# A decoder layer on one core: 192 gathered and 320 dense tokens instead of 128 and 384, with the key search cut into token halves

## The chip, the core and the metric

The kernel runs on one core of one Trainium2 chip. The metric is the device time of one execution in microseconds (us): the median of several runs, beside one execution that the hardware profiler recorded.

## What is computed

One decoder layer on 512 tokens of width 2048, in float32. Attention gives `h1`. The part that the change touches is the retrieval layer behind it: for each token and each of 8 heads two queries score 128 keys each, the best 16 of both are combined, and the best 16 sums name 16 of 16384 experts. A token so has 128 experts with gates.

```python
q = (xt @ wq).reshape(T, PEER_HEADS, 2, PEER_HALF)
s = jnp.einsum('thcd,hcnd->thcn', q, subkeys)
top_s, top_i = lax.top_k(s, PEER_TOPK)
...
u = u_tab[ec]
act = gelu(jnp.einsum('cd,chkd->chk', xc, u))
w = gc * act
return jnp.einsum('chk,chkd->cd', w, v_tab[ec])
```

Then `out = LayerNorm(alpha * h1 + peer + sigmoid(h1 @ ple_gate) * (p @ ple_proj))`.

## The kernel before

**Numbers.** Every product that has to be exact is done in three matmuls (`mm3`, lines 91 to 93): each operand is split into a rounded high part and the rest. `load_split` (81 to 88) does that for weights: SP loads a raw tile of 128x1024 (line 83), ScalarE writes the high part (86), VectorE or, where `eng` says so, GpSimd the low part (87). Raw, high and low tiles rotate over three buffers each. One such load feeds 24 matmuls of the dense stage.

**Tokens.** The 512 tokens stand in 4 blocks `tb` of 128. Block 0 is gathered: its experts' rows are fetched from the u and v tables by an indirect DMA, one expert of each of the 128 tokens at a time, so 128 gathers of u rows and 128 of v rows, each of 128 rows of 8 KB (`gather`, 700; `gather_step`, 708 to 722). VectorE consumes each of them in one instruction: the product with `h1` summed into a column of `act` (711), or the row times its weight added to an accumulator (721). The row tile has two buffers. Blocks 1 to 3 (384 tokens, `TD`) are dense: all 16384 experts are computed for them, with gates that are zero for the experts that were not chosen.

**Stages around the change.**
- `mix`, `norm1`, `spread` (445 to 497): the output matmuls with w_out in two token halves, the first norm, the transposes into the split operand `hs`, and on GpSimd the write of `h1` to DRAM.
- Projection (515 to 525): `p @ ple_proj` in 96 matmuls, written to DRAM as `projd`.
- Key search (586 to 594 and 543 to 584): for each of 16 key sets a query block of 48 matmuls over all 512 tokens, the scores (549), and on VectorE the two rounds of best eight (`top16`, 838 to 843), the sums of pairs and every fourth time the lookup of indices. `experts` (596) makes the softmax gates.
- Gate building (`dense_gates`, 610 to 644): for 24 groups of 16 tokens, one-hot tiles on VectorE, GpSimd and ScalarE, multiplied on TensorE, written to DRAM as `gd`.
- Gate projection (`ple_units`, 646 to 672): `h1 @ ple_gate` in 32 units of 24 matmuls each (512 columns). `fill(n)` (676) issues the next n units; such calls are spread over the end of the key search and the gate building, and `fill(32)` (691) issues what is left.
- Dense stage (763 to 821): 16 rounds g of 8 u blocks (`hp`, line 776, then gelu, gate and split at 779 to 785) and 8 c blocks (`vp`, 807, accumulated at 809 and 811). Every block takes 48 matmuls of 384 columns and ends with `gather_steps()` (727 to 732), which issues as many gather steps as keep them even over the first 240 of 256 blocks.
- The end (823 to 833): second norm, output.

Instructions are traced in the order of the program; the framework orders each engine's instructions by that order and by when its own timing says they are ready. Each engine then runs its queue in order. `issue_after` (730) places the gather's instruction behind the last low-half split on that split's engine.

## Time and profile before

| | us |
|---|---|
| median of 3 runs | 4052.41 |
| lowest and highest run | 4050.92, 4053.77 |
| span of the profiled execution | 4050.8 |
| TensorE busy in it | 3929.8 (97%) |
| VectorE busy | 2531.8 (63%) |
| ScalarE, GpSimd busy | 1318.5 (33%), 639.7 (16%) |

The profiled execution's own time is known by its span, from its first to its last instruction; it lies within 0.1% of the runs. PE is TensorE, PEld its weight loads, DVE VectorE, ACT ScalarE, POOL GpSimd, SP the engine that issues most loads. Busy shares are averages over stages with different limits, so a stage is read by its own window. Recorded matmuls overlap one another: their spacing is read from start to start. PEclk is the clock granted to TensorE as a share of 2.4 GHz.

### The profile page before, as it was taken

To read this page: it belongs to the slowest core of one execution; us is meant where nothing else is said; L and a number is where in the kernel's file an instruction comes from. 1 tells how busy PE (TensorE), PEld (TensorE's weight loads), DVE (VectorE), ACT (ScalarE), POOL (GpSimd) and SP (SyncE) were. 2 spreads that over 40 slices of the span, in tenths; PEclk is the share of its full clock that TensorE was granted. 3 is DMA by queue.
4 is the path that set the end of the run, shared out by engine and by line. 5 is a ranking of instruction groups with operands and counts; after the bars stand their busy time and mean duration, and the time that the engine had idled before them with its cause. 6 is when DMAs were issued, how large, how long until landed. Compare 5 with 4: busy or idle time off the path is not lost.

```text
span 4050.8 us, 52363 instructions
## 1 busy us (share of the span) xinstructions
PE 3929.8 (97%) x20841; PEld 3637.0 (90%) x20841; DVE 2531.8 (63%) x3817; ACT 1318.5 (33%) x1809; POOL 639.7 (16%) x563
## 2 busy tenths in 40 slices
PE   8999999999999897899999999999999999999996
PEld 7888887888887686789999999999999999999996
DVE  5444353322357699986767766666767667766756
ACT  3222233222234321575233223332333233322331
POOL 0000000000002442784111111111111111111101
PEclk9999999999999899899999999999999999999998
DMA  4222222222366422567877777777777777777744
GB/s 145 89 94 86 79 73 75 96 95 96 99 227 205 148 92 67 180 194 230 299 272 276 269 281 273 266 272 277 284 278 265 275 273 279 267 281 263 281 163 150
DMA packets 227588, 801.15 MB, mean 198 GB/s; under 512 B 20624, under 2 KB 71952, under 8 KB 191120
## 3 DMA queue, kind: packets, MB, share of 16 engines
q1 hardware_dynamic: 179856, 483.13, 35.1%
q0 software_dynamic: 40144, 282.09, 19.2%
q10 hardware_dynamic: 7344, 32.59, 2.1%
q8 instruction: 164, 2.69, 0.3%
q14 instruction: 80, 0.66, 0.0%
HBM read 755.78 MB, written 41.94 MB: 197 GB/s over the span
## 4 chain that ended last, share of the span: by engine, by line
PE 86%; DVE 8%; issue 2%; DMA 1%; ACT 1%; POOL 1%; POOLq 0%; DVEq 0%; ACTq 0%; SPq 0%
PE vp L92 9%; PE vp L91 9%; PE vp L93 9%; PE hp L93 9%; PE hp L92 9%; PE hp L91 9%; PE ps_g L92 3%; PE ps_g L91 3%; PE ps_g L93 3%; PE pg L641 2%; PE vps L91 1%; PE vps L92 1%; PE vps L93 1%; PE wo L92 1%; PE wo L93 1%
## 5 line engine op out<-in xcount | busy, mean ns | idle before, releaser
L93 PE MATMUL hp<-m_hi,wlo_u 128*128 128x384 f32 x2048 | 684.2, 334 | 2.5 <-DVE wlo_u L87 2.5
L93 PE MATMUL vp<-ah,wlo_vd 128*128 128x384 f32 x2048 | 685.9, 335 | 0.0
L91 PE MATMUL hp<-m_hi,whi_u 128*128 128x384 f32 x2048 | 684.2, 334 | 0.1
L92 PE MATMUL hp<-m_lo,whi_u 128*128 128x384 f32 x2048 | 684.2, 334 | 0.0
L92 PE MATMUL vp<-al,whi_vd 128*128 128x384 f32 x2048 | 672.4, 335 | 0.0
L91 PE MATMUL vp<-ah,whi_vd 128*128 128x384 f32 x2048 | 670.0, 335 | 0.0
L86 ACT ACTIVATE whi_vd<-raw_vd 128x1024 fp32r<-128x1024 f32 x256 | 271.7, 1061 | 744.5 <-PE vp L92 601.3
L87 DVE TENSOR_TENSOR wlo_u<-raw_u,whi_u 128x1024 fp32r<-128x1024 f32 x256 | 313.2, 1224 | 224.9 <-ACT whi_u L86 221.6
L86 ACT ACTIVATE whi_u<-raw_u 128x1024 fp32r<-128x1024 f32 x256 | 271.4, 1061 | 520.7 <-PE hp L92 401.0
L87 DVE TENSOR_TENSOR wlo_vd<-raw_vd,whi_vd 128x1024 fp32r<-128x1024 f32 x256 | 313.1, 1223 | 203.2 <-ACT whi_vd L86 203.0
L93 PEld LDWEIGHTS hp<-m_hi,wlo_u 128*128 128x128 f32 x2048 | 384.4, 188 | 3.4 <-DVE wlo_u L87 3.4
L91 PEld LDWEIGHTS hp<-m_hi,whi_u 128*128 128x128 f32 x2048 | 384.4, 188 | 0.4 <-ACT whi_u L86 0.4
L92 PEld LDWEIGHTS hp<-m_lo,whi_u 128*128 128x128 f32 x2048 | 384.4, 188 | 0.0
L93 PEld LDWEIGHTS vp<-ah,wlo_vd 128*128 128x128 f32 x2048 | 384.3, 188 | 0.0
L92 PEld LDWEIGHTS vp<-al,whi_vd 128*128 128x128 f32 x2048 | 383.1, 188 | 0.0
L91 PEld LDWEIGHTS vp<-ah,whi_vd 128*128 128x128 f32 x2048 | 382.9, 188 | 0.0
L721 DVE SCALAR_TENSOR_TENSOR accg<-vr,act,accg 128x2048 f32<-128x2048 f32 x128 | 300.3, 2346 | 14.4 <-DMA vr<-in_v_rows,eidx 9.7
L711 DVE SCALAR_TENSOR_TENSOR ur<-ur,h1g 128x2048 f32<-128x2048 f32 x128 | 291.9, 2285 | 15.1 <-DMA ur<-in_u_rows,eidx 15.1
L702 POOL DMA_INDIRECT vr<-in_v_rows,eidx x128 | 143.1, 1118 | 856.9 <-DVE accg L721 826.6
L702 POOL DMA_INDIRECT ur<-in_u_rows,eidx x128 | 140.7, 1100 | 837.6 <-DVE ur L711 821.1
L811 DVE TENSOR_TENSOR acc<-acc,vp 128x384 f32<-128x384 f32 x240 | 130.7, 550 | 131.1 <-PE vp L93 131.1
L91 PE MATMUL ps_g<-x_hi,whi_g 128*128 128x512 f32 x512 | 199.9, 391 | 0.0
(315 smaller groups left out, 6844.6 us busy)
## 6 DMA issues: line engine op xcount, KB each, us to landing
raw_u<-in_u_dense SPq DMA_DIRECT2D x256, 512.0 KB
raw_vd<-in_v_dense SPq DMA_DIRECT2D x256, 512.0 KB
raw_g<-in_w_z SPq DMA_DIRECT2D x64, 512.0 KB
raw_wo<-in_w_out SPq DMA_DIRECT2D x64, 512.0 KB
gd<-sg SPq DMA_DIRECT2D x24, 1024.0 KB
gl<-gd ACTq DMA_DIRECT2D x16, 1536.0 KB
raw_wq<-in_w_q SPq DMA_DIRECT2D x32, 512.0 KB
raw_pg<-in_w_gate SPq DMA_DIRECT2D x32, 512.0 KB
```

Source lines behind the costliest of these rows:

```text
L86: nc.scalar.activation(hi[:, :n], raw[:, :n], AF.Copy)
L87: last_lo[0] = (eng or nc.vector).tensor_sub(lo[:, :n], raw[:, :n], hi[:, :n])
L91: nc.tensor.matmul(ps, whi, mhi, start=start, stop=False, **kw)
L92: nc.tensor.matmul(ps, whi, mlo, start=False, stop=False, **kw)
L93: nc.tensor.matmul(ps, wlo, mhi, start=False, stop=stop, **kw)
L641: nc.tensor.matmul(ps[:, t1 * P:(t1 + 1) * P], o1[:, t1, :], o2, start=True, stop=True)
L702: nc.gpsimd.indirect_dma_start(out=row, out_offset=None, in_=table, in_offset=bass.IndirectOffsetOnAxis(ap=eidx[:, k:k + 1], axis=0))
L711: nc.vector.scalar_tensor_tensor(row, row, 1.0, h1g, op0=ALU.mult, op1=ALU.mult, accum_out=act[:, n:n + 1])
L721: nc.vector.scalar_tensor_tensor(state["acc"], row, act[:, k:k + 1], state["acc"], op0=ALU.mult, op1=ALU.add)
L811: nc.vector.tensor_add(acc[:, db, :], acc[:, db, :], ps[:, :TD])
```

## The change

64 tokens of block 1 (`GX`) leave the dense part and are gathered too. Each stands on two partitions: partition p holds the first half of its experts, partition 64 + p the second, so that 64 more gathers of u rows and 64 of v rows of the same size serve them (`HG` = 192 of each). The two partial sums are added at the end through a 64-row copy. The dense stage has 320 columns, the gate building 20 groups instead of 24.

The key search runs in two halves of 256 tokens, each with its own 16 query blocks of 48 matmuls, and so loads and splits the query weights twice. Gathers begin with half two: two steps behind each of its 16 query blocks, three with every second group of the gate building, the rest spread over the first 240 blocks of the dense stage. The projection moves from its own stage into the ends of the four ple columns, straight from the matmul's bank, and `projd` is gone. `fill` is called in half two, once, and in the gate building; what is left follows it.

```diff
-TD = T - P
+GX = 64
+T0 = P + GX
+TD = T - T0
 NB = TD // 16
+HG = P + P * GX // P
...
-    def column_block(src, act, name, nk=KB, eng=None, pre=()):
+    def column_block(src, act, name, nk=KB, eng=None, pre=(), ts=slice(0, T)):
         ps = bank(f"ps_{name}")
...
-                mm3(ps, hi[:, s], lo[:, s], act[0][:, kb, :], act[1][:, kb, :], kb == 0, kb == nk - 1)
+                mm3(ps[:, :cols], hi[:, s], lo[:, s], act[0][:, kb, ts], act[1][:, kb, ts],
+                    kb == 0, kb == nk - 1)
...
-    y = yp.tile([P, NT, D], F32, name="y")
+    h1g = hp.tile([P, D], F32, tag="h1g", name="h1g")
+    y = [h1g, hp.tile([P, D], F32, tag="h1x", name="y1"),
+         yp.tile([P, D], F32, name="y2"), yp.tile([P, D], F32, name="y3")]
...
+    pre_q = [load_split(w_q[0][:, u * 1024:(u + 1) * 1024], f"wq0_{u}") for u in range(2)]
+    norm1(1)
+    spread(1)
+    s3.close()
+    h1x = hp.tile([P, D], F32, tag="h1x", name="h1x")
+    for i in range(2):
+        nc.scalar.dma_start(h1x[i * GX:(i + 1) * GX, :], h1d[1][0:GX, :])
+
+    ep = s4.enter_context(tc.tile_pool(name="ep", bufs=2))
+    pj_hi = ep.tile([P, 2, T], F32R, name="pj_hi", bufs=1)
...
-    for c in range(4):
-        phi, plo = load_split(w_proj[c], f"pj{c}")
-        for tb in range(NT):
-            ts = slice(tb * P, (tb + 1) * P)
-            pj = bank(f"pj{c}_{tb}")
-            for k in range(2):
-                s = slice(k * 512, (k + 1) * 512)
-                mm3(pj, pj_hi[:, k, ts], pj_lo[:, k, ts], phi[:, s], plo[:, s], k == 0, k == 1)
-            o = xp.tile([P, 512], F32, tag="pj", name=f"pjs{c}_{tb}")
-            nc.scalar.activation(o, pj, AF.Copy)
-            nc.gpsimd.dma_start(projd[tb][:, c * 512:(c + 1) * 512], o)
-
-    pre_q = [load_split(w_q[0][:, u * 1024:(u + 1) * 1024], f"wq0_{u}") for u in range(2)]
-    norm1(1)
-    spread(1)
...
-    def key_scores(hc, q):
-        sk = qp.tile([P, P], F32, tag="sk", name=f"sk{hc}")
+    def key_scores(half, hc, q):
+        tbs = (2 * half, 2 * half + 1)
+        sk = qp.tile([P, P], F32, tag="sk", name=f"sk{half}_{hc}")
         nc.scalar.dma_start(sk, subk[hc])
-        pss = bank(f"pss{hc}")
-        for tb in range(NT):
-            c = slice(tb * P, (tb + 1) * P)
+        pss = bank(f"pss{half}_{hc}")
+        for i in range(2):
+            c = slice(i * P, (i + 1) * P)
             nc.tensor.matmul(pss[:, c], q[:, c], sk, start=True, stop=True)
-        s = qp.tile([P, T], F32, tag="s", name=f"s{hc}")
-        nc.scalar.activation(s, pss, AF.Copy)
-        for tb in range(NT):
-            top16(nc, s[:, tb * P:(tb + 1) * P], tv[:, tb, hc, :], ti[:, tb, hc, :])
+        s = qp.tile([P, 2 * P], F32, tag="s", name=f"s{half}_{hc}")
+        nc.scalar.activation(s, pss[:, :2 * P], AF.Copy)
+        for i, tb in enumerate(tbs):
+            top16(nc, s[:, i * P:(i + 1) * P], tv[:, tb, hc, :], ti[:, tb, hc, :])
         if hc % 2:
             h = hc // 2
-            for tb in range(NT):
+            for tb in tbs:
...
-    prev = None
-    for hc in range(16):
-        ps = column_block(w_q[hc], hs, f"wq{hc}", eng=nc.gpsimd if hc >= 3 else None,
-                          pre=pre_q if hc == 0 else ())
-        q = qp.tile([P, T], F32, tag="q", name=f"q{hc}")
-        nc.scalar.activation(q, ps, AF.Copy)
-        if prev is not None:
-            key_scores(*prev)
-        prev = (hc, q)
-
     def experts(tb):
-        fill(2)
-        gt = lg if tb == 0 else k2.tile([P, HK], F32, tag="gt", name=f"gt{tb}", bufs=3)
+        gt = kp.tile([P, HK], F32, name=f"gt{tb}") if tb else lg[:, 0:HK]
...
+    def gather_step(n):
+        if n < HG:
+            row = gather(n, u_rows, f"ur{n}")
+            nc.vector.scalar_tensor_tensor(row, row, 1.0, h1g if n < HK else h1x, op0=ALU.mult, op1=ALU.mult,
+                                           accum_out=act[:, n:n + 1])
+            return
+        if n == HG:
+            nc.scalar.activation(act, act, AF.Gelu)
+            nc.vector.tensor_mul(act, act, lg)
+            a0 = hp.tile([P, D], F32, tag="h1g", name="accg")
+            nc.gpsimd.dma_start(a0, base[0])
+            ax = hp.tile([P, D], F32, tag="h1x", name="accx")
+            nc.gpsimd.memset(ax[GX:P, :], 0.0)
+            nc.gpsimd.dma_start(ax[0:GX, :], base[1][0:GX, :])
+            state["acc"] = (a0, ax)
+        k = n - HG
+        row = gather(k, v_rows, f"vr{k}")
+        o = state["acc"][k >= HK]
+        nc.vector.scalar_tensor_tensor(o, row, act[:, k:k + 1], o, op0=ALU.mult, op1=ALU.add)
+
+    steps = [0, 0]
+
+    def gather_to(n):
+        while steps[1] < min(n, 2 * HG):
+            with tc.issue_after(last_lo[0].ins):
+                gather_step(steps[1])
+            steps[1] += 1
+
+    picks = {}
+
+    def half_keys(half, early):
+        prev = None
+        for hc in range(16):
+            ps = column_block(w_q[hc], hs, f"wq{half}_{hc}",
+                              eng=nc.gpsimd if hc >= 3 or half else None,
+                              pre=pre_q if not half and hc == 0 else (),
+                              ts=slice(half * 2 * P, (half + 1) * 2 * P))
+            q = qp.tile([P, 2 * P], F32, tag="q", name=f"q{half}_{hc}")
+            nc.scalar.activation(q, ps[:, :2 * P], AF.Copy)
+            if prev is not None:
+                key_scores(half, *prev)
+            prev = (hc, q)
+            if early:
+                gather_to(steps[1] + early)
+        if half:
+            fill(2)
+        key_scores(half, *prev)
+        for tb in (2 * half, 2 * half + 1):
+            picks[tb] = experts(tb)
...
-        tt = k2.tile([P, 3, P], F32, tag="tt", name=f"tt{tb}")
+        tt = k3.tile([P, 3, P], F32, tag="tt", name=f"tt{tb}", bufs=2)
         nc.vector.tensor_copy(tt, ps[:, 0:384].rearrange("p (a t) -> p a t", t=P))
-        for b in range(8):
+        for b in range(GX // 16 if tb == 1 else 0, 8):
             fill(1 if (tb * 8 + b) % 4 else 0)
-            sg = k2.tile([P, P, 16], F32, tag="sg", name=f"sg{tb}_{b}")
+            if (tb * 8 + b) % 2:
+                gather_to(steps[1] + 3)
+            sg = k3.tile([P, P, 16], F32, tag="sg", name=f"sg{tb}_{b}", bufs=2)
...
-            nc.sync.dma_start(gdw[:, :, (tb - 1) * 8 + b, :], sg.rearrange("p (g i) t -> p g (i t)", i=GE))
+            nc.sync.dma_start(gdw[:, :, tb * 8 + b - T0 // 16, :], sg.rearrange("p (g i) t -> p g (i t)", i=GE))
...
-                hi, lo = load_split(w_gate[c][:, u * 1024:(u + 1) * 1024], f"pg{c}_{u}",
-                                    eng=nc.gpsimd if c * 8 + u < 32 else None)
+                hi, lo = load_split(w_gate[c][:, u * 1024:(u + 1) * 1024], f"pg{c}_{u}", eng=nc.gpsimd)
...
+            phi, plo = load_split(w_proj[c], f"pj{c}")
             for tb in range(NT):
-                hr = k2.tile([P, 512], F32, tag="hr", name=f"hr{c}_{tb}")
+                ts = slice(tb * P, (tb + 1) * P)
+                pj = bank(f"pj{c}_{tb}")
+                for k in range(2):
+                    s = slice(k * 512, (k + 1) * 512)
+                    mm3(pj, pj_hi[:, k, ts], pj_lo[:, k, ts], phi[:, s], plo[:, s], k == 0, k == 1)
+                hr = ep.tile([P, 512], F32, tag="hr", name=f"hr{c}_{tb}")
                 nc.sync.dma_start(hr, h1d[tb][:, cs])
-                pj = k2.tile([P, 512], F32, tag="pj", name=f"pjr{c}_{tb}")
-                nc.sync.dma_start(pj, projd[tb][:, cs])
-                sg = k2.tile([P, 512], F32, tag="psg", name=f"psg{c}_{tb}", bufs=4)
+                sg = ep.tile([P, 512], F32, tag="psg", name=f"psg{c}_{tb}")
                 nc.scalar.activation(sg, ps[tb], AF.Sigmoid)
                 nc.vector.tensor_mul(sg, pj, sg)
                 nc.vector.scalar_tensor_tensor(sg, hr, ALPHA, sg, op0=ALU.mult, op1=ALU.add)
...
-    fill(2)
-    key_scores(*prev)
-    fill(1)
-    picks = [experts(0)]
-    ef = k2.tile([P, HK], F32, tag="ef", name="ef")
-    nc.vector.scalar_tensor_tensor(ef, picks[0][0], 128.0, picks[0][1], op0=ALU.mult, op1=ALU.add)
-    nc.vector.tensor_copy(eidx, ef)
-    for tb in range(1, NT):
-        picks.append(experts(tb))
+    half_keys(0, 0)
+    ef = k2.tile([P, 2, HK], F32, tag="ef", name="ef", bufs=1)
+    for tb in range(2):
+        nc.vector.scalar_tensor_tensor(ef[:, tb, :], picks[tb][0], 128.0, picks[tb][1], op0=ALU.mult, op1=ALU.add)
+    nc.vector.tensor_copy(eidx[:, 0:HK], ef[:, 0, :])
+    for i in range(P // GX):
+        ps_, ks = slice(i * GX, (i + 1) * GX), slice(i * GX, (i + 1) * GX)
+        nc.vector.tensor_copy(eidx[ps_, HK:HG], ef[0:GX, 1, ks])
+        nc.vector.tensor_copy(lg[ps_, HK:HG], picks[1][2][0:GX, ks])
+    half_keys(1, 2)
+    sq.close()
+    k3 = s4.enter_context(tc.tile_pool(name="k3", bufs=3))
     for tb in range(1, NT):
         dense_gates(tb)
     fill(32)
...
-    steps = [0, 0]
+    calls = [0, steps[1]]
 
     def gather_steps():
-        steps[0] += 1
-        while steps[1] < min(2 * HK, steps[0] * 2 * HK // (NG * 16 - 16)):
-            with tc.issue_after(last_lo[0].ins):
-                gather_step(steps[1])
-            steps[1] += 1
+        calls[0] += 1
+        gather_to(calls[1] + calls[0] * (2 * HG - calls[1]) // (NG * 16 - 16))
...
-                    mm3(ps[:, :TD], hi[:, s], lo[:, s], hs[0][:, kb, P:T], hs[1][:, kb, P:T],
+                    mm3(ps[:, :TD], hi[:, s], lo[:, s], hs[0][:, kb, T0:T], hs[1][:, kb, T0:T],
                         kb == 0, kb == KB - 1)
...
-                        nc.tensor.transpose(ps[:, i * P:(i + 1) * P],
-                                            acc[:, 2 * c - 2 + i, (tb - 1) * P:tb * P], ident)
+                        nc.tensor.transpose(ps[:k, i * P:(i + 1) * P],
+                                            acc[:, 2 * c - 2 + i, tb * P + lo_ - T0:tb * P + hi_ - T0], ident)
...
-            for c in range(4):
-                nc.vector.bn_stats(st2[:, 0, c, :], state["acc"][:, c * 512:(c + 1) * 512])
-            stats2(0, 1)
-            finish(state["acc"], 0, 0, D, False)
+            a0, ax = state["acc"]
+            up = rp.tile([P, D], F32, tag="row", name="up")
+            nc.sync.dma_start(up[0:GX, :], ax[GX:P, :])
+            nc.vector.tensor_add(ax[0:GX, :], ax[0:GX, :], up[0:GX, :])
+            for st, zt, dst in ((0, a0, out_rows[0]), (NT, ax[0:GX, :], out_rows[1][0:GX, :])):
+                for c in range(4):
+                    nc.vector.bn_stats(st2[:zt.shape[0], st, c, :], zt[:, c * 512:(c + 1) * 512])
+                stats2(st, st + 1)
+                finish(zt, st, dst, 0, D, False)
```

## Rows read from the trace of the kernel before

**Rows 1.** Windows by stage: us, busy us (instructions) per engine, PEclk, DMA share, GB/s
```profile
1313.70:1347.00 33.30, 29.20 (x131) 22.21 (x129) 18.10 (x34) 19.47 (x34) 8.91 (x17) 0.92 0.70 238
1347.00:1385.30 38.30, 30.44 (x110) 23.54 (x110) 25.72 (x20) 8.78 (x15) 20.93 (x7) 0.76 0.32 112
1385.30:1556.00 170.70, 165.20 (x771) 137.53 (x770) 158.19 (x648) 41.16 (x53) 68.13 (x28) 0.99 0.28 92
1556.00:1657.50 101.50, 75.82 (x315) 60.30 (x314) 100.66 (x340) 21.92 (x27) 30.62 (x15) 0.88 0.30 94
1657.50:1876.00 218.50, 204.99 (x1228) 181.70 (x1229) 178.81 (x453) 169.77 (x316) 189.76 (x219) 0.95 0.64 188
1900.00:1950.00 50.00, 47.43 (x269) 46.17 (x268) 38.55 (x42) 17.66 (x25) 11.44 (x8) 1.00 0.84 308
1950.00:3870.00 1920.00, 1920.00 (x11079) 1920.00 (x11078) 1339.19 (x1291) 590.54 (x688) 270.99 (x247) 1.00 0.76 274
```
**Rows 2.** Costliest groups of the page: busy us, mean ns, idle before and its releaser
```profile
L93 PE MATMUL hp<-m_hi,wlo_u 128*128 128x384 f32 x2048 | 684.2, 334 | 2.5 <-DVE wlo_u L87 2.5
```
**Rows 3.** Timeline of TensorE: start us, us (x8: all eight), line, operation, tile
```profile
900.03 0.39 PE L91 MATMUL ps_g<-x_hi,whi_g 128*128 128x512 f32 x1
902.75 0.39 PE L91 MATMUL ps_g<-x_hi,whi_g 128*128 128x512 f32 x1
...
2500.06 0.34 PE L91 MATMUL vp<-ah,whi_vd 128*128 128x384 f32 x1
2509.76 0.34 PE L91 MATMUL vp<-ah,whi_vd 128*128 128x384 f32 x1
...
1880.64 0.33 PE L91 MATMUL hp<-m_hi,whi_u 128*128 128x384 f32 x1
...
4018.64 1.47 PE L816 MATMUL zt<-ident,acc 128*128 128x128 f32 x12
...
1556.27 1.05 PE L549 MATMUL pss<-sk,q 128*128 128x128 f32 x8
```
**Rows 4.** Groups by line and form, VectorE, then one group of GpSimd
```profile
L87 DVE TENSOR_TENSOR wlo_u<-raw_u,whi_u 128x1024 fp32r<-128x1024 f32 x256 | 313.2, 1224 | 224.9 <-ACT whi_u L86 221.6 <-issue 2.9 <-PE hp L93 0.4
L721 DVE SCALAR_TENSOR_TENSOR accg<-vr,act,accg 128x2048 f32<-128x2048 f32 x128 | 300.3, 2346 | 14.4 <-DMA vr<-in_v_rows,eidx 9.7 <-DMA accg<-base 4.5
L711 DVE SCALAR_TENSOR_TENSOR ur<-ur,h1g 128x2048 f32<-128x2048 f32 x128 | 291.9, 2285 | 15.1 <-DMA ur<-in_u_rows,eidx 15.1
L811 DVE TENSOR_TENSOR acc<-acc,vp 128x384 f32<-128x384 f32 x240 | 130.7, 550 | 131.1 <-PE vp L93 131.1
L785 DVE TENSOR_TENSOR al<-a,ah 128x384 fp32r<-128x384 f32 x128 | 71.5, 559 | 70.5 <-ACT ah L784 70.5
...
L87 POOL TENSOR_TENSOR wlo_wq<-raw_wq,whi_wq 128x1024 fp32r<-128x1024 f32 x26 | 64.3, 2477 | 118.2 <-ACT whi_wq L86 97.7 <-PE pss L549 20.4
```
**Rows 5.** The gathered row tile ur
```profile
DMA to landing us min/median/max: 5.3/5.6/10.9
```
**Rows 6.** Timeline of GpSimd and of VectorE from 1918 us
```profile
1918.53 1.68 POOL L702 DMA_INDIRECT ur<-in_u_rows,eidx  x1 [6.29 <-DVE ur L711]
1929.40 1.68 POOL L702 DMA_INDIRECT ur<-in_u_rows,eidx  x1 [5.52 <-DVE ur L711]
...
1926.83 2.29 DVE L711 SCALAR_TENSOR_TENSOR ur<-ur,h1g 128x2048 f32<-128x2048 f32 x1 [2.14 <-DMA ur<-in_u_rows,eidx]
```
**Rows 7.** DMA queues from 2500 to 3500 us
```profile
q0 software_dynamic: 18582, 135.31, 37.6%
q1 hardware_dynamic: 34770, 126.59, 35.4%
```
**Rows 8.** Windows of ten microseconds, columns as in rows 1
```profile
1960.00:1970.00 10.00, 10.00 (x60) 10.00 (x59) 7.22 (x10) 2.44 (x3) 0.94 (x1) 1.00 0.93 360
```
**Rows 9.** Waits from 1380 to 1660 us: total us, times, longest
```profile
ACT h1g_gate L601 <- DVE h1g_gate L600: 26.7, 1, 26.7
```

103 lines of the change are left out of this document (47 added, 56 removed).

## The prediction

> **What bounds the kernel now.** I read the busy times of each engine by stage first [rows 1]. In the dense stage (first hp matmul at 1880.64, last transposes behind it at 4018.64 us [rows 3]) TensorE is busy in every microsecond at the full granted clock (1.00, the 2.4 GHz level), while VectorE is at 70% and the 16 DMA engines at 0.76. So TensorE alone sets the end there, and what an instruction of it takes is the price of the stage. The groups by line say the same from the other side: 2048 hp matmuls of one line waited 2.5 us in all [rows 2]. The stage ahead of it is another matter. From 1385 to 1657 us (key search) VectorE is busy 158.2 of 170.7 and 100.7 of 101.5 us, and TensorE is idle for 26 us of the second stretch at clock 0.88: VectorE bounds the search. In the gate building after it (1657.5 to 1876) TensorE (205 of 218.5 us), VectorE (179), ScalarE (170) and GpSimd (190) are all nearly full [rows 1]. So the change takes work from an engine that is the bound for 2138 us, and gives work to VectorE and the DMA queues, which bound elsewhere.
>
> **Part A, columns of the dense matmuls.** There are 12288 of them (6 groups of 2048, of which one stands in [rows 2]), 48 in each step of the stage (a u block or a c block, called a call below). Starts lie (902.75 - 900.03) / 12 = 226.7 ns apart at 512 columns and (2509.76 - 2500.06) / 56 = 173.2 ns at 384 [rows 3]. The slope is 53.5 / 128 = 0.418 ns a column, one column per 2.4 GHz cycle, over a fixed 13 ns. No 320-column matmul is in the trace. The line gives 146.5 ns; the bounds are 173.2 (no gain, if the weight load of each matmul were the floor) and 111 ns (8 matmuls of 128 columns, each with its own weights, start in (1.05 - 0.27) / 7 ns steps [rows 3], the 0.27 being one of them by itself). I take the line, since the two nearest rows lie on it. Saved: 26.7 x 12288 = 328 us; a call falls from 8.31 to 7.03 us.
>
> The Trainium skill (TensorE: Matmul & The Clock Gate, section Back-to-back issue gap) speaks against this: sustained spacing there is about 81 ns at 128 columns and 131 ns at 512, so by our estimate from that page 64 columns are worth 8.3 ns, part A 102 us, and the whole sum would end near 4080 us. The trace disagrees at 512 columns, with 226.7 ns, so the measurement is used.
>
> **Part B, more gathers in a shorter stage.** Steps go from 256 to 384 (192 for u, 192 for v). Two with each of 16 key blocks of half two and three with every second of the 20 gate groups make 32 + 30 = 62 before the dense stage; 322 are spread over 240 of its 256 calls. At 7.03 us a call these last 1687 us, so one gather is due every 5.24 us, where now it is 240 x 8.31 / 256 = 7.8 us.
> VectorE first. A call holds two splits (1.22 us), two 384-column operations (0.55; at 320 columns 0.48) and 1.34 gathers (2.29 and 2.35) [rows 4]: 2.45 + 0.96 + 3.1 = 6.5 of 7.03 us. It fits, with only half a microsecond left for waits.
> Then the gather's own chain. Two row buffers: gather n+2 is issued when VectorE has consumed n. At the quiet rate a gather lands 5.6 us after issue [rows 5], so two per 5.6 + 2.3 + 0.3 = 8.2 us, 4.1 each, and nothing is lost. But one stretch of this trace runs at nearly the new rate. From 1900 to 1950 us DMA is at 0.84 and 308 GB/s [rows 1], a gather issued at 1918.53 is consumed at 1926.83 after VectorE stood 2.14 us for it, and its buffer is issued again at 1929.40 [rows 6]: two gathers per 10.87 us, 5.44 each. TensorE lost 2.6 us in those 50 [rows 1]. That is the near row, and it says 322 x 5.44 = 1752 us, 65 more than 1687. The demand would be higher still: 322 gathers of 1 MiB and 240/256 of 268 MB of dense weights and 21 MB of gates are 609 MB in 1687 us, 361 GB/s, and the highest ten microseconds I found moved 360 at share 0.93 [rows 8]; queue by queue, 274 GB/s now cost 37.6 + 35.4% and a little [rows 7], which also scales to about 360 at full share. So I take 5.5 us: 1771, a loss of **84 us**. Ends: 0 (the quiet landing) and, with the longest landing of 10.9 us [rows 5], (10.9 + 2.6) / 2 = 6.75 us each, a loss of 487. Behind a late gather on VectorE's queue stand the next split's low half and the accumulation; TensorE, whose three weight buffers hold two blocks of 3.5 us, waits for the former.
>
> The Trainium skill (DMA: Bandwidth & Descriptors, section Specifications) gives about 358 GB/s as a core's HBM limit; by that alone part B would be 609 MB / 358 = 1701 us, a loss of 14, and the sum 3868 us. The ten-microsecond row at 360 agrees with it as a ceiling.
>
> **Part C, the stage ahead.** Steps, from 1313.7 us (end of the w_out matmuls) on:
> The projection (96 matmuls, 21.8 us by the 512-column pitch, with 16 evacuations and 16 GpSimd stores) leaves the front, where the second norm's transposes stood behind it on TensorE. Keys can start on VectorE at 1363 instead of 1385. The 16 reads of the projection on SP go too.
> Query matmuls: 1536 at 256 columns instead of 768 at 512. By the line 119.9 ns, 184 us instead of 174. VectorE's search covers the 10 us; without that cover they cost 10. 32 more weight splits on ScalarE and GpSimd (2.4 us each there [rows 4]) lie under the same cover.
> The search itself is the same work, 272 us [rows 1], now in two halves. Half two carries 32 gathers, 32 x 2.29 = 73 us more on VectorE. On GpSimd a gather waits for VectorE to free its row, with the low halves of later query weights behind it; they have a full key block of slack. Half one's end holds ScalarE for VectorE's softmax, as the 26.7 us wait does today [rows 9]: 0 to 27 us, taken as 8, since splits already done cover most.
> Gate building: 218.5 / 24 = 9.1 us a group now; VectorE's share is 7.45 and becomes 7.45 + 1.5 x 2.3 = 10.9, GpSimd's 7.9 becomes 9.5. I take 12 (that plus the present tenth of waits), 20 groups: 240 us; bounds 10.9 and 13.5.
> Gate projection (ple) units: 17 of 32 are issued by then, 15 remain, and two projection blocks: 17 x 24 x 226.7 ns = 92 us, with no gather beside them. Some will slip into TensorE's gaps between groups; I take 50, bounds 15 and 92.
> Sum: 1363 + 272 + 73 + 8 + 240 + 50 = 2006, against the dense stage's start at 1880.6: **+125 us**. Ends: 1941 (+60) and, without the earlier start, 1385 + 272 + 73 + 27 + 270 + 92 = 2119 (+238).
>
> **Part D, the end.** Finishing the 64 extra tokens adds a 64-row copy and some 10 us of VectorE, in the last 16 calls, which hold no gathers: taken as +5, between 0 and 15.
>
> **Sum.** Profiled span 4050.8 - 328 + 84 + 125 + 5 = 3937. The median of the runs is 1.6 above that span, so **3938 us**.
>
> **Rivals.**
> Forecast: faster, 3860 to 4020 us; 0.64.
> Gathers keep pace: B is 0 and C about +80 because ple units fill the gate building: 3808 us. For it: average DMA share 0.76 and 4.1 us quiet. Against: the 1900 to 1950 stretch. 0.18.
> Slower: the two-buffer gather chain becomes the bound. The point is 5.24 + (328 - 125 - 5) / 322 = 5.86 us a gather, a landing of 9.1 us. At 6.2 us B is 309 and the time 4163 us. For it: 8.3 us landings at only 308 GB/s; against: the peak of 360 was reached without TensorE standing. 0.12.
> The matmul's spacing does not follow its columns: A about 102 us, then 7.9 us calls, B 0, about 4080 us. Against: the 384- and 512-column rows. 0.03.
> Terms that cancel within 0.2% (8 us, what a measurement of this kernel can tell from no change): 0.03. That the early gathers do not come early is excluded by their place in VectorE's order; that they only stall it there is in C.
>
> So faster 0.64 + 0.18 = 0.82, same 0.03, slower 0.15. The range leaves out the lowest part of the second case and the slower cases but their edge: 3830 to 4055 us.
>
> **What the changed profile would show.** Right: dense matmuls 146 to 147 ns apart; the first hp matmul near 2006 us; waits of VectorE for gathers growing from 15.1 + 9.7 us [rows 4] to well over 100, TensorE idle between 50 and 120 us there, DMA share above 0.9. Wrong: spacing above 150 ns, a dense start beyond 2080 or before 1940, TensorE without idle time, or landings past 9 us.

## The result, and the profile after it

| | before | after |
|---|---|---|
| median of 4 runs, us | 4053.09 (4050.92 to 4054.92) | 4118.44 (4109.18 to 4138.49) |
| profiled span, us | 4050.8 | 4113.1 |
| first hp matmul | 1880.6 | 2107.9 |
| last transpose zt | 4019.8 | 4081.9 |

The ratio of the runs is 1.0167, 95% interval 1.0141 to 1.0193: slower by 1.7%, where 2.8% faster was forecast. The spans split the difference: the dense stage (first hp to last zt) fell from 2139.2 to 1974.0 us, 165 less; the stage ahead of it grew by 227 us; the end is the same within 1 us. The sum is 62 us.

TensorE in the dense stage of the changed kernel (timeline; to compare with [rows 3]):

```profile
2602.32 0.31 PE L96 MATMUL vp<-ah,wlo_vd 128*128 128x320 f32 x1
...
2604.96 0.31 PE L96 MATMUL vp<-ah,wlo_vd 128*128 128x320 f32 x1
```

Eighteen steps from start to start in 2.64 us are 146.7 ns each; the line through 512 and 384 columns had said 146.5. The matmuls gave what was hoped. What stands between them is in the costliest groups of the page (to compare with [rows 2]):

```profile
L96 PE MATMUL hp<-m_hi,wlo_u 128*128 128x320 f32 x2048 | 641.0, 314 | 43.5 <-DVE wlo_u L90 43.2
```

and in the waits of the dense stage from 2109 to 4022 us (total us, times, longest):

```profile
PE vp L96 <- DVE wlo_vd L90: 54.4, 31, 4.3
PE hp L96 <- DVE wlo_u L90: 43.2, 30, 4.2
...
DVE ur L607 <- DMA ur<-in_u_rows,eidx: 91.4, 59, 5.2
...
DVE accg L622 <- DMA vr<-in_v_rows,eidx: 64.9, 39, 4.7
DVE accx L622 <- DMA vr<-in_v_rows,eidx: 43.8, 31, 4.0
...
ACT whi_vd L89 <- DMA raw_vd<-in_v_dense: 382.3, 120, 8.6
...
ACT whi_u L89 <- DMA raw_u<-in_u_dense: 168.3, 94, 7.7
```

ScalarE's two waits for weights before, from 1881 to 4020 us:

```profile
ACT whi_vd L86 <- DMA raw_vd<-in_v_dense: 23.1, 6, 8.1
ACT whi_u L86 <- DMA raw_u<-in_u_dense: 11.9, 4, 6.0
```

TensorE waits about 110 us, nine tenths of it for low halves of weights from VectorE. VectorE waits 200 us for rows (25 before [rows 4]), and ScalarE 551 us for dense weights that have not landed (35 before). The stages, in windows (columns as in [rows 1]):

```profile
1347.00:1385.70 38.70, 7.11 (x39) 6.74 (x38) 18.77 (x16) 6.72 (x11) 14.43 (x6) 0.59 0.42 138
1385.70:1557.20 171.50, 143.49 (x1089) 140.76 (x1089) 162.56 (x566) 56.10 (x84) 102.37 (x42) 0.90 0.46 141
1557.20:1772.00 214.80, 111.89 (x670) 101.02 (x669) 212.32 (x486) 38.81 (x55) 100.85 (x59) 0.77 0.66 220
1772.00:2024.20 252.20, 182.94 (x950) 159.38 (x951) 211.85 (x440) 136.91 (x258) 221.62 (x210) 0.84 0.79 253
2024.20:2107.90 83.70, 83.70 (x372) 69.32 (x371) 14.56 (x16) 20.43 (x22) 28.90 (x16) 1.00 0.46 139
2107.90:4081.90 1974.00, 1860.08 (x12337) 1837.94 (x12335) 1572.00 (x1520) 646.24 (x777) 406.94 (x327) 0.98 0.87 321
```

In order: a stretch ahead of the keys in which TensorE does 7 us of work in 39; half one; half two with VectorE busy 212 of 215 us; the gates; a tail of 84 us in which TensorE is full and VectorE busy for 15; the dense stage. The border between the halves is drawn where half one's indices are done; by then VectorE has begun half two (40 of 64 MAX8 first selections lie ahead of it, and 32 are half one's), so the two are safest read as a sum, 386.3 us. In the search several of VectorE's operations are longer than before (groups from 1385 to 1775 us, mean ns after the busy us):

```profile
L581 DVE TENSOR_TENSOR oh<-oh,tf 128x512 f32<-128x512 f32 x32 | 45.4, 1442 | 0.0
...
L574 DVE CAST bcf<-bc 128x64 f32<-128x64 uint32 x16 | 18.3, 1149 | 0.0
L883 DVE FIND_INDEX8 ti<-tv,s 128x8 uint32<-128x128 f32 x64 | 17.5, 280 | 0.0
```

The same three before:

```profile
L582 DVE TENSOR_TENSOR oh<-oh,tf 128x512 f32<-128x512 f32 x32 | 32.5, 1033 | 0.0
...
L843 DVE FIND_INDEX8 ti<-tv,s 128x8 uint32<-128x128 f32 x64 | 17.4, 282 | 0.0
...
L575 DVE CAST bcf<-bc 128x64 f32<-128x64 uint32 x16 | 8.5, 532 | 0.0
```

The product oh went from 1033 to 1442 ns and the cast bcf from 532 to 1149, while FIND_INDEX8 stayed at 280. Not every product grew: oh from bcf and io went from 928 to 815. Beside them GpSimd ran 57 subtractions wlo_wq of 2539 ns (144 us) where it ran 26 (64 us).

### The profile page after: what moved, and what is told of

The parts are those of the page before. It is cut to its first block, busy times and chain, and to the rows that moved or that the text cites. A ratio compares the mean times of both kernels' runs of the same rounds, so it can differ in the third digit from the quotient of the medians.

```text
span 4113.1 us, 54046 instructions
## 1 busy us (share of the span) xinstructions
PE 3688.2 (90%) x21481; PEld 3403.4 (83%) x21481; DVE 2794.2 (68%) x3954; ACT 1308.4 (32%) x1812; POOL 914.5 (22%) x677
## 4 chain that ended last, share of the span: by engine, by line
issue 18%; PE 17%; DVE 14%; DMA 12%; POOL 5%; ACT 0%; POOLq 0%; DVEq 0%; ACTq 0%
DMA vr<-in_v_rows,eidx 6%; POOL ur L600 4%; PE hp L96 3%; PE hp L94 3%; PE hp L95 3%; PE vp L96 2%; PE vp L94 2%; DVE ur L607 2%; PE vp L95 2%; DMA ur<-in_u_rows,eidx 2%; DMA raw_vd<-in_v_dense 2%; DMA raw_u<-in_u_dense 1%; DVE oh L581 1%; DVE accx L622 1%; DVE wlo_u L90 1%
## 5 line engine op out<-in xcount | busy, mean ns | idle before, releaser
L96 PE MATMUL hp<-m_hi,wlo_u 128*128 128x320 f32 x2048 | 641.0, 314 | 43.5 <-DVE wlo_u L90 43.2
L96 PE MATMUL vp<-ah,wlo_vd 128*128 128x320 f32 x2048 | 612.4, 315 | 56.6 <-DVE wlo_vd L90 56.6
L94 PE MATMUL vp<-ah,whi_vd 128*128 128x320 f32 x2048 | 633.4, 314 | 13.5 <-ACT whi_vd L89 13.5
L94 PE MATMUL hp<-m_hi,whi_u 128*128 128x320 f32 x2048 | 638.1, 312 | 0.2 <-ACT whi_u L89 0.2
L95 PE MATMUL hp<-m_lo,whi_u 128*128 128x320 f32 x2048 | 637.7, 311 | 0.0
L95 PE MATMUL vp<-al,whi_vd 128*128 128x320 f32 x2048 | 632.4, 313 | 0.0
L600 POOL DMA_INDIRECT vr<-in_v_rows,eidx x192 | 244.2, 1272 | 851.6 <-DVE accg L622 533.2
L600 POOL DMA_INDIRECT ur<-in_u_rows,eidx x192 | 233.3, 1215 | 733.5 <-DVE ur L607 671.0
L607 DVE SCALAR_TENSOR_TENSOR ur<-ur,h1g 128x2048 f32<-128x2048 f32 x128 | 307.1, 2399 | 78.3 <-DMA ur<-in_u_rows,eidx 78.1
L689 PE MATMUL pg<-o,o 128*128 128x128 f32 x640 | 113.6, 336 | 150.5 <-ACT o L685 91.6
```

Source lines behind the costliest of these rows:

```text
L94: nc.tensor.matmul(ps, whi, mhi, start=start, stop=False, **kw)
L95: nc.tensor.matmul(ps, whi, mlo, start=False, stop=False, **kw)
L96: nc.tensor.matmul(ps, wlo, mhi, start=False, stop=stop, **kw)
L600: nc.gpsimd.indirect_dma_start(out=row, out_offset=None, in_=table, in_offset=bass.IndirectOffsetOnAxis(ap=eidx[:, k:k + 1], axis=0))
L607: nc.vector.scalar_tensor_tensor(row, row, 1.0, h1g if n < HK else h1x, op0=ALU.mult, op1=ALU.mult, accum_out=act[:, n:n + 1])
L689: nc.tensor.matmul(ps[:, t1 * P:(t1 + 1) * P], o1[:, t1, :], o2, start=True, stop=True)
```

## The experiments

The kernel before took 4050 to 4057 us beside each of them. The change, e6, e7 and g1 have four runs, the others one; the four of the change lie 29 us apart, so a smaller difference between single runs says little. The texts for d1, s1, e1 and e2 count 52 gathers ahead of the dense stage or 332 in it; the right numbers are 62 and 322. Their 542 us of waits for weights in the change are those of a shorter window than the 551 above. "Dense" is the first hp to the last zt.

| run | us | dense start | dense |
|---|---|---|---|
| the change | 4118.4 | 2107.9 | 1974.0 |
| d1 no row transfers in dense | 3954.7 | 2106.1 | 1815.5 |
| d2 no gather operation in dense | 3995.0 | 2100.1 | 1861.8 |
| d3 three row buffers | 4053.8 | 2102.3 | 1918.2 |
| d4 rows of half width | 3956.9 | 2107.0 | 1816.8 |
| d5 five weight buffers | 4151.6 | 2113.2 | 1898.6 |
| s1 no early gathers | 3929.1 | 1935.3 | 1965.0 |
| f1 gating early | 4069.0 | 2059.1 | 1976.6 |
| f2 no low query weights | 4027.0 | 2024.6 | 1968.7 |
| f3 early memory | 4114.7 | 2093.5 | 1988.1 |
| e1 all gathers in dense | 4144.7 | 1936.6 | 1994.3 |
| e2 the same, three rows | 3986.2 | 1938.7 | 2014.0 |
| e4 unsplit search, as e2 | 3936.8 | 1875.2 | 2028.6 |
| e5 as e4, gating early | 3933.4 | 1866.7 | 2033.6 |
| e6 as e5, four weight buffers | 3878.7 | 1867.7 | 1962.0 |
| e7 as e5, 32 added tokens | 3912.2 | 1897.8 | 1990.1 |
| g1 the change, 3 rows, 4 weights | 4019.1 | 2104.9 | 1881.2 |

### The dense stage: what holds TensorE

**d1.** In the dense stage the rows are two tiles of zeros:

```diff
     def gather(k, table, name):
+        if "still" in state:
+            return state["still"][k % 2]
```

> The changed kernel, with the row transfers of the dense stage left out: its 332 gather operations on VectorE run on two rows of zeros that stay in place, so the output lacks the gathered experts. Theory L (the dense stage waits because a gather has only two row buffers, and each row comes over 8 us after its issue): the wait is gone, the dense stage falls from 1973 us to 1810-1840 and the program to some 3960 us. Theory D (weights and rows together fill the DMA engines, and the weights come late): the same, and the waits of ScalarE for dense weights (542 us in the changed kernel) fall below 60 us. Theory V (VectorE, 80% busy, holds the weight halves back behind its 2.3 us gather operations): the dense stage stays above 1930 us and the program above 4070 us.

The window of the dense stage:

```profile
2106.10:3921.60 1815.50, 1809.02 (x12337) 1807.12 (x12335) 1555.74 (x1520) 642.73 (x777) 5.00 (x7) 1.00 0.53 165
```

1815.5 us, TensorE busy 1809: the floor of this stage. So the transfers cost 158.5 us, and VectorE at 1556 us of work does not bound it by itself: theory V in its plain form falls.

**d2.** The transfers stay, the operations on VectorE go (both `scalar_tensor_tensor` of `gather_step` are skipped in the dense stage).

> The changed kernel, with the gather operations on VectorE left out in the dense stage and the row transfers kept, so the output lacks the gathered experts. Theory L: a row buffer is free as soon as its row has landed, two gathers in 8 us or so, under the 5.2 us at which they are due, so the dense stage falls to 1810-1850 us and the program to some 3970 us. Theory D: the traffic is as before or comes faster, the dense stage stays above 1920 us, the waits of ScalarE for dense weights stay above 400 us. Theory V: VectorE falls to about half busy, the dense stage to 1810-1850 us, and TensorE's waits for VectorE there (98 us) go.

The windows of the dense stage and of 1000 us in it, then ScalarE's waits from 2101 to 3902 us:

```profile
2100.10:3961.90 1861.80, 1832.54 (x12336) 1810.32 (x12335) 879.92 (x1067) 645.42 (x776) 328.30 (x305) 1.00 0.87 330
2500.00:3500.00 1000.00, 984.00 (x6616) 970.34 (x6615) 461.04 (x554) 342.84 (x409) 232.95 (x215) 1.00 0.99 384
...
ACT whi_vd L89 <- DMA raw_vd<-in_v_dense: 429.3, 170, 8.0
...
ACT whi_u L89 <- DMA raw_u<-in_u_dense: 214.2, 107, 5.4
```

1861.8 us, between all the forecasts. ScalarE still waits 643 us for weights, yet TensorE waits only 27 us for low halves and high halves together, so late weights alone do little. The operations, and the waits for rows that stand before them on VectorE, cost the other 112 us; d2 takes away both and doesn't part them. That a late weight has no slack left to stand behind a gather operation is a reading that fits, not shown by itself. Rows and weights also ran at 384 GB/s for a whole millisecond, on the same two row and three weight buffers: the 321 GB/s of the change were not the most that the DMA engines can bring.

**d3.** A third row buffer in the dense stage:

```diff
-        row = rp.tile([P, D], F32, tag="row", name=name)
+        if "row" in state and k % 3 == 2:
+            row = state["row"].tile([P, D], F32, tag="row3", name=name)
+        else:
+            row = rp.tile([P, D], F32, tag="row", name=name)
```

> The changed kernel with a third row buffer for the gathers of the dense stage, everything else as it is. Theory L: a gather has half as much time again, VectorE's waits for rows (197 us) fall below 60 us and the dense stage falls by 80 us or more, to 1890 us or less; the program to some 4030 us. Theory D: the dense stage stays within 30 us of 1973 us, and the rows land later than before (10 us or more from issue) as three are under way. Theory V: the dense stage stays within 30 us of 1973 us too, with VectorE's waits for rows gone and TensorE's waits for VectorE still there.

56 us back, short of the 80 that theory L named. The waits of the dense stage in d3 (all of those for rows that are listed, then those for weights):

```profile
DVE ur L610 <- DMA ur<-in_u_rows,eidx: 5.5, 1, 5.5
...
ACT whi_vd L89 <- DMA raw_vd<-in_v_dense: 438.4, 165, 9.5
ACT whi_u L89 <- DMA raw_u<-in_u_dense: 281.8, 125, 7.3
```

The waits for rows are gone and those for weights grew from 551 to 720 us. So the third row gives back a third of the loss, and what is left (103 us) is a loss with late weights and without waits for rows.

**d4.** Each transfer brings 1024 columns; VectorE reads them twice, so its operation keeps its length (`table.rearrange("n (a w) -> (n a) w", w=1024)`, the row broadcast over two halves).

> The changed kernel with rows of half the width in the dense stage: each transfer brings 1024 columns of 128 rows, 0.5 MB and not 1 MB, and VectorE's operation reads them twice, so that it takes its 2.3 us; the output's gathered experts are wrong data. Without the transfers the dense stage took 1815 us, with them 1974. Theory D (bytes: weights and rows together need the DMA engines 0.87 of the time): 322 half rows take 170 MB off 602 MB, the dense stage falls to 1815-1850 us. Theory L (latency of two buffers): a landing of half the bytes comes in some 5 us and not 8, the stage falls as far. Theory Q (each gather costs by its 128 descriptors and its issue on GpSimd, and not by bytes): the stage stays above 1930 us. The waits of ScalarE for weights tell D from L: under D below 150 us, under L they stay near 540 us.

The window of d4's dense stage:

```profile
2107.00:3923.80 1816.80, 1809.66 (x12336) 1807.16 (x12335) 1558.31 (x1519) 643.44 (x777) 369.77 (x326) 1.00 0.77 257
```

and its waits there:

```profile
ACT whi_u L89 <- DMA raw_u<-in_u_dense: 18.0, 8, 3.2
ACT whi_vd L89 <- DMA raw_vd<-in_v_dense: 16.7, 7, 4.5
```

The floor again, with every gather issued and every operation of VectorE in place, and ScalarE's waits for weights down to 35 us, which theory D asked and theory L did not. So it is the size of the rows; their number, issue and descriptors on GpSimd (theory Q) cost nothing here. VectorE's waits for rows fell too, from 200 to 37 us; d4 doesn't tell whether the rows help as fewer bytes beside the weights or by landing sooner in their own chain.

**d5.** Two more buffers for raw weights, rows on two as before:

```diff
+        loads[0] += 1
+        if more[0] and loads[0] % 5 > 2:
+            raw = more[0].tile([P, 1024], F32, tag="raw2", name=f"raw_{name}")
+        else:
+            raw = wp.tile([P, 1024], F32, tag="raw", name=f"raw_{name}")
-        raw = wp.tile([P, 1024], F32, tag="raw", name=f"raw_{name}")
```

> The changed kernel with five buffers for the raw weights of the dense stage and not three, the rows on two as before. Theory P (the weights come late because a buffer of theirs is freed only by VectorE's low half, which stands behind gather operations that wait for rows, so that too few loads are under way): with two more loads ahead, ScalarE's waits for weights (542 us) halve and the dense stage falls by 40 us or more, to 1930 us or less. Theory D (the DMA engines are full and share themselves out between weights and rows): the rows land later in return, and the dense stage stays within 25 us of 1974 us.

The dense matmuls took 75 us less, and the program 33 us more. ScalarE's waits for weights fell from 551 to 26 us. Rows (q0) and weights (q1) that d5 moved from 2500 to 3500 us (packets, MB, share):

```profile
q0 software_dynamic: 23259, 169.31, 44.8%
q1 hardware_dynamic: 39879, 145.22, 41.1%
```

the tile accx of d5, whose row ends with the first and last start of its gather operations:

```profile
L628 DVE SCALAR_TENSOR_TENSOR accx<-vr,act,accx x64: 2275/2352/2355, 3747.2 to 4127.5; 128x2048 f32<-128x2048 f32 x64
```

and the queues in the changed kernel (to compare with [rows 7], where they were 135 and 127 MB):

```profile
q0 software_dynamic: 25019, 182.11, 48.8%
q1 hardware_dynamic: 37156, 135.30, 36.3%
```

In the same 1000 us the weights gained 10 MB and the rows lost 13: a row of 1 MiB every 5.76 us became one every 6.19, and the last gather operation started 116 us after the last transpose. Both theories are half right: more loads under way free TensorE (P), and the rows pay for it (D). The total was 328.8 MB in the change and 327.4 here. This is the rival's mechanism, the two-buffer chain as the end of the program, in the open.

### The stage ahead: where 227 us come from

**s1.** The early gathers are left out (`gather_to` counts them without issuing before the dense stage).

> The changed kernel with the 52 gathers ahead of the dense stage left out (transfers and VectorE operations; the output lacks these experts), the dense stage as it is. By the prediction's prices for them (73 us in the second half of the key search, and some 55 us of operations and waits in the gate building, where VectorE is 84% busy) the dense stage starts 90-130 us earlier than 2108, at 1980-2020 us. If they lie beside other work, it starts less than 30 us earlier. The tail of the token gating after the gates (84 us) stays in either case, and the dense stage takes 1973 us within 20.

Half one, half two, the gates and the tail of s1:

```profile
1385.90:1554.50 168.60, 144.83 (x1094) 142.10 (x1094) 158.91 (x567) 56.23 (x84) 102.92 (x42) 0.90 0.47 144
1554.50:1680.50 126.00, 108.02 (x660) 97.35 (x658) 125.93 (x419) 32.39 (x48) 60.96 (x25) 0.93 0.38 113
1680.50:1850.00 169.50, 154.50 (x948) 136.90 (x949) 140.88 (x379) 138.04 (x263) 148.06 (x181) 0.96 0.64 187
1850.00:1935.30 85.30, 85.30 (x378) 70.59 (x378) 14.54 (x16) 20.46 (x23) 29.39 (x17) 1.00 0.45 136
```

173 us earlier, more than expected. Half two is 126 us and not 215 (32 gathers, 89 us: 2.8 each), the gates 170 and not 252 (30 gathers, 83 us: 2.8 each). VectorE is full in half two (212 of 215 us), where an early gather so costs its whole operation and some waiting. In the gates VectorE is busy 212 and GpSimd, which issues the gathers, 222 of 252 us (141 and 148 of 170 in s1); which of them sets the price there was not separated. In the dense stage of the changed kernel it costs 158.5 / 322 = 0.5 us.

**e1, e2.** What the 62 cost when they are moved into the dense stage, on two and on three row buffers:

```diff
-    half_keys(1, 2)
+    half_keys(1, 0)
...
-            if (tb * 8 + b) % 2:
-                gather_to(steps[1] + 3)
```

> The changed kernel with no gather ahead of the dense stage: all 384 are spread over its 240 calls, on two row buffers. The run without early gathers started the dense stage at 1935 us, so this one does too, within 15. Theory L (each gather takes a place in the two-buffer chain, 5.76 us apart in the changed kernel): 384 of them need 2210 us, and the program takes some 4180 us. Theory S (a gather in the dense stage costs what it shares with the other work, (1974 - 1815) / 332 = 0.48 us, against 173 / 52 = 3.3 us ahead of it): the dense stage takes 1815 + 184 = 2000 us, the program some 3965 us.

> The same with a third row buffer in the dense stage. Theory S with the price of the run with three rows, (1918 - 1815) / 332 = 0.31 us a gather: dense stage 1935 us, program 3900 us. Theory D (weights and rows fill the DMA engines; 384 rows of 1 MB and the weights of 256 MB at the 331 GB/s that the run with three rows reached): 403 MB + 268 MB at 331 GB/s is 2030 us, program some 3990 us. Theory V (VectorE: 808 us of other work and 384 x 2.3 us are 1691 us, with waits for the weights between them): above 2030 us.

The last window of e1, from the last transpose to the end:

```profile
3930.90:4142.60 211.70, 0.45 (x3) 0.05 (x1) 124.28 (x83) 4.75 (x8) 58.30 (x47) 0.50 0.64 221
```

and its tile accx:

```profile
L622 DVE SCALAR_TENSOR_TENSOR accx<-vr,act,accx x64: 2276/2352/2402, 3791.8 to 4120.2; 128x2048 f32<-128x2048 f32 x64
```

TensorE's part of the stage took 1994 us, as theory S said to 6 us; the program took 4145, near theory L's 4180: TensorE is not held by a chain that is late, it ends and waits 212 us for it. With a third row the gathers keep up, the end is 31 us as ever, and the program is at 3986, 68 us below the kernel before. The dense stage is then 2014 us, near theory D's 2030 and far over theory S's 1935: its price of 0.31 us a gather did not carry from 322 gathers to 384.

**f2.** The low half of the query weights is left out (no `wlo_wq`, no third matmul for it).

> The changed kernel with the low half of the query weights left out (GpSimd's 57 subtractions of 2.5 us and the third matmul of each product; the queries lose low bits). Theory G (GpSimd's subtractions hold up VectorE's operations in the key search): the means of VectorE's operations in the halves fall to those of before (cand 612 ns from 797, oh 1033 from 1442, tf 599 from 1095), the first half takes 130-140 us and not 170, the dense stage starts 35-60 us earlier. If VectorE's operations are longer for another reason: the halves stay as they are, within 10 us.

Windows of f2, to the start of the keys and of its two halves:

```profile
1347.00:1367.10 20.10, 5.42 (x24) 5.16 (x25) 10.93 (x11) 7.43 (x12) 7.70 (x4) 0.62 0.64 213
1367.10:1505.00 137.90, 134.02 (x1092) 131.63 (x1092) 132.90 (x629) 80.84 (x116) 9.33 (x5) 0.99 0.79 258
1505.00:1676.40 171.40, 48.19 (x186) 37.78 (x186) 169.38 (x423) 15.49 (x22) 49.41 (x40) 0.65 0.67 227
```

and its groups from 1385 to 1775 us:

```profile
L585 DVE TENSOR_TENSOR oh<-oh,tf 128x512 f32<-128x512 f32 x32 | 20.4, 679 | 0.0
...
L887 DVE FIND_INDEX8 ti<-tv,s 128x8 uint32<-128x128 f32 x57 | 15.6, 284 | 0.0
...
L578 DVE CAST bcf<-bc 128x64 f32<-128x64 uint32 x16 | 5.0, 314 | 0.0
```

Half one is 137.9 us (171.5 in the change), the product oh 679 ns (1442), the cast 314 (1149), FIND_INDEX8 284: the operations lengthen when GpSimd works beside them, and only some kinds do. Of the 83 us by which the dense stage comes earlier, 77 lie in the two halves (309.3 us for 386.3), 19 in the start of the keys, and the gates and the tail take 12 back. This is the price of all 57 subtractions; the price of the 31 that the change added was not measured. The third matmul went too, but TensorE was not what half two waited for: it was busy 112 of 215 us in the change. The Trainium skill (SBUF — State Buffer, section Who interferes with whom) says that VectorE and GpSimd share one pair of ports under an exclusive lock, and that VectorE operations with two SBUF inputs, or in a two-port mode, contend for it. The rows agree: from f2 to the change the products of two tiles and the casts grow, and FIND_INDEX8 doesn't.

**f3.** The query tiles in memory that nothing earlier holds, the projection's input split later.

```diff
+    qp = s4.enter_context(tc.tile_pool(name="qp", bufs=2))
     s3 = ExitStack()
...
+            if not half and hc == 2:
+                ...
+                nc.scalar.activation(pj_hi, rv, AF.Copy)
```

> The changed kernel with the query tiles in memory that no earlier tile holds, and the split of the projection's input moved behind the third query block (and six and not eight buffers for the gates' second factor, to make room). Between the end of the mix and the first key operation on VectorE (1347 to 1386 us) TensorE is busy 7 us of 39 in the changed kernel. If ScalarE's wait for the memory of the freed rows makes that hole: keys on VectorE start at 1360-1368 us as the prediction had it, and the dense stage starts 15-25 us earlier than 2108. If the hole is the load and low half of the query weights behind the row spreading on GpSimd: it stays, within 5 us.

In the change ScalarE stood for memory that the store of the rows still held, in the waits from 1347 to 1386 us:

```profile
ACT pj_hi L530 <- DMA h1d<-y: 12.2, 1, 12.2
```

With f3 the keys start on VectorE at 1364.3 (1385.7 in the change; 1363 was predicted) and the dense stage at 2093.5, 14 us earlier. Memory is one part of the cause. The store was late because it stood on GpSimd behind a subtraction of query weights, in the change:

```profile
1367.90 2.34 POOL L90 TENSOR_TENSOR wlo_wq<-raw_wq,whi_wq 128x1024 fp32r<-128x1024 f32 x1 [9.88 <-ACT whi_wq L89]
1370.18 1.12 POOL L501 DMA_DIRECT2D h1d<-y  x2
```

In f2, which has no such subtraction, it was issued at 1353.6, ScalarE did not wait for it, and the keys started at 1367.1 with the tiles placed as in the change. The program of f3 is as long as it was (4114.7): the dense stage took 14 us more. That is within the 29 us by which the runs of the change differ, and was not followed up.

**f1.** One gating unit after each query block of half two (`if half: fill(1)`), against the tail.

> The changed kernel with one unit of the token gating after each of the 16 query blocks of the second half, where TensorE is busy 114 of 218 us, so that nothing is left behind the gate building. Theory W (VectorE's work sets the pace of the halves and the gates, and the 84 us tail is work of TensorE that could lie beside it): the tail goes, the second half grows by 15 us at most, the dense stage starts at 2025-2045 us, the program takes some 4045 us. Theory G (the weights' low halves on GpSimd and the two engines in each other's way set the pace): the second half grows by 40 us or more, and the dense stage starts after 2060 us.

The tail went (84 us), the two halves grew from 386 to 441 us (half two alone from 215 to 284), the gates fell from 252 to 234; the dense stage starts 49 us earlier, at 2059. Theory W missed, theory G was nearer: the units bring GpSimd 16 more subtractions into a stretch that VectorE bounds. How much of the 54 us is theirs was not separated.

### What beats both

**e4, e5.** Only the added tokens: the keys in one pass of 512 tokens as before, all gathers in the dense stage, three row buffers (e4); gating units after each query block (e5).

> Of the change only the 64 added tokens: 320 tokens in the dense stage, all 384 gathers there on three row buffers, the keys searched in one pass of 512 tokens as in the kernel before; the projection stays in the token gating. Dense stage 2014 us as in the run with all gathers there and three rows. If the split of the key search into halves costs what the stage ahead lost beside the early gathers (query weights loaded and split twice, GpSimd beside VectorE): the gates have 20 blocks and not 24 at 9 us each, so the dense stage starts at 1850-1890 us, and the program takes 3895-3935 us. If the split costs nothing, it starts at 1939 us as there, and the program takes 3985 us.

> The same, with one unit of the token gating after each query block (16 in the search and 2 at its end) and none between the experts' gates. If VectorE's work sets the pace up to the gates and TensorE has 100 us to spare in the search (272 us of VectorE's work beside 175 us of matmuls): dense stage 20-40 us earlier than in the kernel it is made from. If TensorE sets it, the same within 10 us; if GpSimd's further subtractions hold VectorE up, later by 10 us or more.

e4 starts the dense stage at 1875.2 against 1938.7 in e2, as far ahead as was expected, but not for the split alone: its gates start 30 us earlier (1654.2 against 1683.8), which is the search, and the other 34 are the gating units that e4, like the kernel before, issues between the experts' gates and that e2 leaves to the tail. Its dense stage took 2028.6, 15 more than e2's. e5 gains 8.5 us at the start, of the 20 to 40 expected, and loses 5 of them again; "the same within 10 us" is what came, and single runs don't tell more.

**e6, e7.** e5 with a fourth buffer for raw weights, and e5 with 32 added tokens (`GX = 32`).

> The unsplit kernel with early gating and three row buffers, now with four buffers for the raw weights of the dense stage. There TensorE waits 144 us in 2034 for weights whose loads come late. Theory P (too few weight loads under way): dense stage 1930-1980 us, program 3840-3880 us, rows still in time on three buffers. Theory D (DMA engines 0.90 busy at 343 GB/s; weights and rows are 268 + 403 MB, 1956 us at that rate): TensorE's part of the stage falls, to 1960-2000 us, but the gathers then end after it, and the program stays above 3900 us.

> The unsplit kernel with early gating and three row buffers, with 32 added tokens and not 64 (each on four partitions; 320 gathers, 352 tokens in the dense stage). By theory D the dense stage with 64 is bound by bytes (671 MB at 343 GB/s is 1956 us, matmuls 1815 us) and with 32 by matmuls: a pitch of 160 ns, between 146.7 at 320 and 173.2 at 384 columns, times 12288 is 1966 us, bytes 268 + 336 MB at 343 GB/s are 1760 us. So TensorE's waits fall from 144 us below 40, dense stage 1975-2010 us, two more blocks of gates 10-20 us: program 3900-3925 us. If VectorE's gather operations cost TensorE by themselves and not by late bytes (320 and not 384 of them), the waits stay above 90 us and the program is slower than with 64, above 3945 us.

The dense window of e5:

```profile
1866.70:3900.30 2033.60, 1884.75 (x12343) 1836.03 (x12343) 1699.05 (x1638) 648.85 (x778) 580.39 (x386) 0.98 0.90 343
```

of e6:

```profile
1867.70:3829.70 1962.00, 1853.64 (x12344) 1826.78 (x12343) 1686.09 (x1628) 639.28 (x777) 550.09 (x385) 0.99 0.93 356
```

and of e7:

```profile
1897.80:3887.90 1990.10, 1984.18 (x12344) 1982.50 (x12343) 1581.29 (x1542) 655.29 (x777) 455.60 (x322) 1.00 0.85 318
```

e6 takes 3878.7 us, 0.957 of before (0.9556 to 0.9588). The dense stage of 1962 fits both theories, the program only P: one more load under way raises the rate from 343 to 356 GB/s, and the gathers end nearly with the stage (the end behind it is 42 us, against 31 where they end ahead of it). e7 takes 3912.2 us, 0.965 (0.963 to 0.967): with 64 gathers (67 MB) less its stage is matmuls alone, 1984 of 1990 us. ScalarE still waits over 400 us there for weights, so again late weights alone do not hold TensorE. Bytes and operations fell together, so e7 doesn't tell which of them held e5. Its dense stage starts 31 us later than e5's where 10 to 20 were expected; that was not followed up.

**g1.** The change as it is, with d3's third row and e6's fourth weight buffer.

> The changed kernel as it is up to the dense stage, with three row buffers and four buffers for the raw weights there. If the buffers alone keep the DMA engines from what they can bring (356 GB/s in the run with both): TensorE's waits of 110 us fall below 40, the dense stage from 1974 to 1835-1870 us, the gathers end in time (322 and not 384), and the program takes 3970-4010 us, below the kernel before although the stage ahead is 227 us later. If 62 early gathers less in it change little, and the stage is held by VectorE: above 1920 us, program above 4055 us.

The dense window of g1:

```profile
2104.90:3986.10 1881.20, 1826.11 (x12336) 1814.29 (x12335) 1566.30 (x1519) 647.02 (x777) 499.60 (x326) 0.99 0.89 337
```

4019.1 us, 0.992 of before (0.990 to 0.993), 9 us above what was expected (the dense stage 11), TensorE waiting 51 us where 40 were named: 12 KB a partition of buffers turn the change from 1.7% slower to 0.8% faster, with the stage ahead still 224 us later.

## Why the prediction was wrong

**Part A was right.** 328 us were predicted; d1, where nothing else stands in the stage, gives 2139.2 - 1815.5 = 323.7. The estimate from the Trainium skill (TensorE: Matmul & The Clock Gate, section Back-to-back issue gap), 102 us, is refuted by the 146.7 ns above.

**Part B failed in size and half in mechanism.** 84 us were predicted, 158.5 measured (1974.0 - 1815.5), within its ends. The gathers ran at 5.76 us each from 2500 to 3500 us (1000 us for 182.11 MB), over the 5.5 taken and under the 5.86 at which the rival decides. In the sum's own terms this is the mis-sized one: 322 x 5.76 - 1687 is 168. It is about what the two-row chain can give, since e1, where a gather is due every 4.9 us, ran at 5.79 (181.14 MB). But the loss was priced as that chain alone. d3 takes it away and gets 56 us back; in the rest the dense weights come late beside the rows, which no term held. It takes VectorE's operations as well: d2, without them and with weights as late, loses 46 us. [Rows 7] showed the two queues at 37.6 and 35.4% and were used for a ceiling on the sum; they were not asked what the weights' own landing would do with three buffers. The sentence on the Trainium skill (DMA: Bandwidth & Descriptors, section Specifications) set the loss by 358 GB/s at 14 us; here 321 GB/s were reached with three weight and two row buffers and 356 with four and three (e6), and 384 over 1000 us with three and two where VectorE read no rows (d2). So neither that figure nor the 360 of [rows 8] was a ceiling here; the measurement decides.

**Part C failed**, +227 us for +125, inside its end of +238. Term by term:
- Keys start at 1363: they started at 1385.7, 23 us late. The new tiles lie in memory that the rows' store still held; f3 has 1364.3. The prediction followed neither what each tile's memory waits for nor where the store stands on GpSimd.
- The search in 272 + 8 us without its gathers: 294.6 in s1, 15 late. The 32 more weight splits were to "lie under the same cover". GpSimd had the time (busy 102 of 171.5 us in half one), but its subtractions lengthen VectorE's operations: without any of the 57 subtractions the halves take 309.3 us with their gathers, and not 386.3 (f2).
- The 32 gathers of half two in 73 us: 91.7 (386.3 - 294.6), 19 late.
- Gates 240: 252.2, 12 late.
- Tail 50: 83.7, 34 late, near the end of 92 named. TensorE was busy 183 of 252 us in the gates, and no gating unit moved into the rest.

These are 22.7 + 14.6 + 18.7 + 12.2 + 33.7 = 101.9 us, all that lies between 125 and 227. **Part D** was 5 and is 0.

Against the profiled span: 4050.8 - 323.7 + 158.5 + 227.3 + 0.2 = 4113.1.

**The slower rival** named the row chain as the bound at 6.2 us a gather. It came near in time (4163) and not in cause: of the 176 us that the sum missed, 102 are the stage ahead and 75 the waits of the dense stage. The chain itself is real: it ends the program in d5 and e1. The case of gathers that keep pace is refuted by 200 us of waits for rows. Of the signs named: spacing 146.7 ns, TensorE idle about 110 us and gather waits over 100 us came as named; a dense start beyond 2080, named as wrong, came too, and the DMA share stayed at 0.87 where above 0.9 was named.
